# A gated short-convolution layer on one core: in-place scaling in the head, a folded -1/2, small products one chunk earlier, and a halved last store

## The chip, the core and the metric

The kernel runs on one core of a Trainium2 chip. The metric is the device time of one execution in microseconds (us), the median of several runs. Engines are named as the profile names them: PE is TensorE (matmuls; PEld its weight loads), DVE is VectorE, ACT is ScalarE, POOL is GpSimd, and SP is SyncE, which issues the DMAs. The engines run side by side; each works through its own instructions in the order in which the program lists them, and waits on semaphores of the others.

## The reference

With DEPTH = 1 only the first kind of layer runs, on x of 1024 rows by 1024 columns, in float32:

```
u  = x * rsqrt(mean(x*x) + 1e-6) * pre_norm
z, bg, cg, v = split(u @ w_in, 4)              # w_in: 1024 x 8192, each part 2048 wide
y  = bg * causal_conv3(cg * v, conv_w) * silu(z)
m  = y @ w_out                                 # w_out: 2048 x 1024
out = x + m * rsqrt(mean(m*m) + 1e-6) * post_norm
```

## The kernel before, in words

**Precision.** Each float32 operand is split into a high part (ScalarE, a rounding copy, L154) and a low part (VectorE, source minus high part, L155). A product of two operands is three matmuls: low by high, high by low, high by high (L188 to L190).

**Fewer products.** Both matrix products are cut into 2 x 2 blocks and done with seven block products instead of eight, called a to g. The sums of blocks that they need are made on POOL (`add_s`, L146 to L150, for the input weights: `se`, `sc`, `sf`, and `d` in place) and on VectorE and POOL for u. ScalarE and VectorE then split them.

**Chunks and pairs.** The first matmul is done in 16 chunks of 128 inner channels. A chunk c is two pairs, p = 2c (parts CG and V) and p = 2c + 1 (parts Z and BG), so chunk 2, the third, is pairs 4 and 5. For each pair the main loop (L790) issues products c, e, d, f of the pair, product a of the next pair, and g; the list `slots` (L742 to L757) holds the order. Up to chunk DEEP - 1 product b of the next pair also stands in it. From chunk DEEP on the two products b of a chunk are replaced by a second level of the same scheme: seven small products a' to g' of half the depth and 256 columns (`deep_product`, L670), spread among the others.

**What the small products need.** Once, the blocks of u's part b are rebuilt on POOL (`deep_parts`, L612, four adds of 512 columns), combined on POOL (`deep_subs`, L618, eight subtractions of 256) and split by ScalarE and VectorE (`deep_split`, L629: c', e', d', g'). The table `UNDER` (L760) says after which product each of these is issued. For each chunk POOL also makes four half sums of weights (`deep_sums`, L642), which `deep_prep` splits.

**Order of the work around it.** `prepare` (L780) issues the weight splits of every product that starts within LEAD = 7 us of the end of the current one, by a clock of 2.72 us a product and 0.72 a small one. `after` (L203) issues what follows a product: copies out of PSUM (`snap`, ScalarE), sums (VectorE: L212, L215, L220), SiLU, the gates (POOL: L217, L223, L225) and, at g, the last step of the convolution's input and the convolution (L236, L578, L581). Then come `add_s` of the next pair at e, d and f, the DMA loads `fetch(p + 2)` at d, and the entry of `UNDER`. Buffers are 36 pages of 128 x 512; the DMAs all go through SP's queue in program order.

**Head** (L410 to L470). The rows of x are eight tiles of 128. For each of the first four, ScalarE sums the squares, `rstd_start` and `rstd_finish` make 1/rms (a square root, a reciprocal and one Newton step: L103 to L111, with -1/2 times the reciprocal as an operation of its own, L105), and VectorE writes a diagonal matrix of it (`dg`, L420). TensorE turns the 128 x 128 blocks of the tile (L345) by a matmul with that diagonal, which scales in the same step. Some half tiles are scaled in place instead, by POOL (L425) and ScalarE (L433), and turned with the identity (L347). `high` and `low` (L357, L360) then read the turned blocks, times the norm's weight `gcol`, into the two parts of u_a and u_b. The first products (`plain`, L390 to L392) run on these without the seven-product scheme, with four turns of blocks between them. The second four tiles are squared, scaled in place (L468, L470) and turned later (`turn2`, L483). `rebuild` (L407) adds u's parts together on POOL. `stir` (L321) issues idle matmuls.

**Output** (L851 to L971). The second matmul runs in the same seven products over halves; rows of the result are normed, scaled with `gpost`, added to the residual `xr` (`finish`, L902) and stored, 256 KB at a time (L889).

Of the kernel before, what the change touches and what calls it, by code (L numbers as in the profile page):

```python
# [11 lines left out]
AF = mybir.ActivationFunctionType  # L12
ALU = mybir.AluOpType
EPS = 1e-6
WARM = 14
PAGES = 36
DEEP = 3
LEAD = 7.0


# [1 line left out]
def kernel(  # L22
# [16 lines left out]
    nc = tc.nc  # L39
    P = 128  # L40
    _, L, D = x.shape
    CI = w_out.shape[1]
    NT = L // P
    NK = D // P
    NC = CI // P
    HB = 512
    NE = D // HB
    TAPS = conv_w.shape[1]
    KH = NK // 2
    TH = NT // 2  # L50
# [4 lines left out]
    of = out.rearrange("b l d -> (b l) d")  # L55
# [12 lines left out]
    def bank(name):  # L68
        return psum.tile([P, HB], F32, tag="bank", name=name)

    def page(name, dtype=F32, shape=(HB,)):

        return pages.tile([P, *shape], dtype, tag="pg", name=name, bufs=PAGES)
# [4 lines left out]
    ident = const.tile([P, P], F32, tag="ident", name="ident")  # L78
# [16 lines left out]
    def rstd_finish(started, more=EPS):  # L95

        sd, ss, name, n = started

        def col(tag):
            return small.tile([P, n], F32, tag=f"{tag}{n}", name=f"{tag}_{name}")  # L100

        ve, r0, nt, hr, rs = (col(tag) for tag in ("ve", "r0", "nt", "hr", "rs"))
        nc.vector.tensor_scalar(ve, ss, more, None, op0=ALU.add)  # L103
        nc.vector.reciprocal(r0, sd)
        nc.vector.tensor_scalar(hr, r0, -0.5, None, op0=ALU.mult)  # L105
        if n == 1:
            nc.vector.scalar_tensor_tensor(nt, r0, ve, r0, op0=ALU.mult, op1=ALU.mult)
        else:
            nc.vector.tensor_mul(nt, r0, r0)
            nc.vector.tensor_mul(nt, nt, ve)  # L110
        nc.vector.scalar_tensor_tensor(rs, nt, 3.0, hr, op0=ALU.subtract, op1=ALU.mult)  # L111
        return rs


# [5 lines left out]
    def fetch(p, rows=(0, 1)):  # L120

        if p >= len(PAIRS):
            return
        c, tys = PAIRS[p]
        for n in rows:
            c0 = tys[n] * CI + c * P
            for k in (0, 1):
                if (p, n, k) not in raws:
                    raws[p, n, k] = page(f"raw_{p}_{n}{k}", shape=(KH, P))
                nc.sync.dma_start(raws[p, n, k], wiv[:, k * KH : (k + 1) * KH, c0 : c0 + P])  # L130
# [72 lines left out]
    def after(p, i):  # L203
# [22 lines left out]
        elif i == "g":  # L226
            if p % 2:
# [3 lines left out]
                y_done(c, cvs.pop(c))  # L231
            elif c < DEEP:
                start_conv(c)

    def start_conv(c, beside=lambda: None):
        nc.vector.tensor_mul(gpad[:, TAPS - 1 : TAPS - 1 + HB], banks[2 * c, "x"], sn[2 * c, "a"])  # L236
        conv(c, beside)
# [4 lines left out]
    def y_done(c, cv):  # L242
        nc.sync.dma_start(y_d[:, c], cv)
        done[c] = cv
# [54 lines left out]
    xs = [xa[:, t] for t in range(TH)] + [xb[:, t] for t in range(TH)]  # L299
# [2 lines left out]
    junk = page("junk", BF16, (D,))  # L302
    sq = small.tile([P, NT], F32, tag="sq", name="sq", bufs=1)
    gcol = small.tile([P, NK], F32, tag="gcol", name="gcol", bufs=1)
    dg = page("dg", shape=(TH, P))

    def load_x(t):
        nc.sync.dma_start(xs[t], xf[t * P : (t + 1) * P, :])
# [10 lines left out]
    def stir(n):  # L319
        for _ in range(n):  # L320
            nc.tensor.matmul(pw[:, :P], idle, idle, start=True, stop=True, skip_group_check=True)  # L321
# [16 lines left out]
    def turn(k, t):  # L338

        if (k, t // TH) not in pk:  # L340
            pk[k, t // TH] = bank(f"pk_{k}_{t // TH}")
        dst = pk[k, t // TH][:, t % TH * P : (t % TH + 1) * P]
        src = xs[t][:, k * P : (k + 1) * P]
        if t < 2 or t < TH and k < KH:
            nc.tensor.matmul(dst, src, dg[:, t], start=True, stop=True, skip_group_check=True)  # L345
        else:
            nc.tensor.transpose(dst, src, ident)  # L347

    def col(k):

        return xb[:, :, k * P : (k + 1) * P]
# [19 lines left out]
            plain_w[p, n, k] = [page(f"wn{n}{k}{h}_{p}", F32R) for h in "hl"]  # L371
            nc.scalar.copy(plain_w[p, n, k][0], block(p, n, k))

    def low_plain(p, n):
        for k in (0, 1):
            hi, lo = plain_w[p, n, k]
            nc.vector.tensor_sub(lo, block(p, n, k), hi.bitcast(F32))

# [32 lines left out]
    for t in range(TH):  # L411
        square(t)
        if t == 0:
            fetch(0)
            for t2 in range(TH, NT):
                load_x(t2)
            fetch(1)
            nc.sync.dma_start(cw_rows, conv_w[0].rearrange("t (c p) -> (t c) p", p=P))
        rs = pre_rstd([t])
        nc.vector.tensor_scalar(dg[:, t], ident, rs, None, op0=ALU.mult)  # L420
        for k in range(NK - 1 if t < 2 else KH):
            turn(k, t)
        late = xs[t][:, KH * P :]
        if t == 2:
            nc.gpsimd.tensor_scalar(late, late, rs, None, op0=ALU.mult)  # L425
        if t == 0:
            pg = pw[:, P : P + NK]
            nc.tensor.transpose(pg, grow, ident[:NK, :NK])
        if t == 1:
            nc.vector.tensor_copy(gcol, pg)  # L430
            stir(2)
    high_plain(0, 0)
    nc.scalar.activation(late, late, AF.Copy, scale=rs)  # L433
    low_plain(0, 0)

    def read_k(k):
        i, kk = "ab"[k // KH], k % KH
# [4 lines left out]
        read_k(k)  # L442
    high_plain(0, 1)
    low_plain(0, 1)
    fetch(2)
    for k in range(KH):
        plain(0, 0, 0, 0, [k], first=k == 0)
        for t in (2, 3) if k < KH - 1 else range(TH):
            turn(k + KH, t)
    read_k(4)  # L450
    square(TH)
# [157 lines left out]
    HH, KQ = HB // 2, KH // 2  # L609
    deep, deep_w = {}, {}  # L610

    def deep_parts(ks):  # L612

        for k in ks:
            deep[k] = page(f"deep{k}")
            nc.gpsimd.tensor_add(deep[k], UH["b"][:, k].bitcast(F32), UL["b"][:, k].bitcast(F32))

    def deep_subs(ks):  # L618

        for k in ks:  # L620
            (b11, b12), (b21, b22) = ((t[:, :HH], t[:, HH:]) for t in (deep[k], deep[k + KQ]))
            nc.gpsimd.tensor_sub(b12, b12, b11)
            nc.gpsimd.tensor_sub(b22, b22, b12)
            nc.gpsimd.tensor_sub(b11, b22, b11)
            nc.gpsimd.tensor_sub(b21, b21, b22)
# [117 lines left out]
    for p in range(2, len(PAIRS)):  # L743
        q = p + 1
        more = p // 2 >= DEEP
        sub = {"c": "a'", "e": "b'", "f": "c'", "a": "e'"} if p % 2 == 0 else {"c": "f'", "e": "d'", "f": "g'"}
# [4 lines left out]
        if q <= END:  # L751
            slots.append(("a", q))
            if more and p % 2 == 0:
                slots.append((sub["a"], p // 2))
            if q // 2 < DEEP:
                slots.append(("b", q))
# [1 line left out]


    UNDER = {  # L760
        ("c", 2 * DEEP - 2): lambda: deep_parts([0]),
        ("e", 2 * DEEP - 2): lambda: deep_parts([2]),
        ("d", 2 * DEEP - 2): lambda: deep_parts([1]),
        ("f", 2 * DEEP - 2): lambda: deep_parts([3]),
        ("g", 2 * DEEP - 2): lambda: deep_subs([0]),
        ("c", 2 * DEEP - 1): lambda: deep_subs([1]),
        ("a", 2 * DEEP): lambda: (deep_split("c'"), deep_split("e'")),
        ("g", 2 * DEEP - 1): lambda: deep_split("d'"),
        ("c", 2 * DEEP): lambda: deep_split("g'"),
# [3 lines left out]
    at, t = [], 0.0  # L773
# [78 lines left out]
    gpost = [page(f"gpost{e}") for e in range(NE)]  # L852
    for e in range(NE):
        nc.sync.dma_start(gpost[e], post_norm[:, e * HB : (e + 1) * HB].broadcast_to([P, HB]))
    gx = [page(f"gx{q}") for q in range(TH)]
    acc = p2.tile([P, 2, TH, HB], F32, tag="acc", name="acc")
    jk = p2.tile([P, HB], BF16, tag="jk", name="jk")
# [25 lines left out]
    def load_res(t):  # L883
        xr[t] = [page(f"xr{t}{e}") for e in range(NE)]
        for e in range(NE):
            nc.sync.dma_start(xr[t][e], xf[t * P : (t + 1) * P, e * HB : (e + 1) * HB])

    def store(t, e, src):
        nc.sync.dma_start(of[t * P : (t + 1) * P, e * HB : (e + 1) * HB], src)  # L889
# [12 lines left out]
    def finish(t):  # L902
        early = 0 if t < TH else 1
        late = 1 - early
        o, r = halves_of(t), xr[t]
        gl = gpost[late]
        ss, sl = sums_of[t], so[:, t, late : late + 1]
        sd = small.tile([P, 1], F32, tag="sd1", name=f"sd_post{t}")
        nc.scalar.activation(sd, sl, AF.Sqrt, bias=ss)
        if t < TH:  # L910
            rs = rstd_finish((sd, sl, f"post{t}", 1), ss)
            z = o[late]
            nc.vector.scalar_tensor_tensor(z, z, rs, gl, op0=ALU.mult, op1=ALU.mult)  # L913
            nc.gpsimd.tensor_add(z, z, r[late])  # L914
        else:
            z = gx[t - TH]
            nc.vector.tensor_mul(z, o[late], gl)
            rs = rstd_finish((sd, sl, f"post{t}", 1), ss)
            nc.vector.scalar_tensor_tensor(z, z, rs, r[late], op0=ALU.mult, op1=ALU.add)
            store(t, late, z)  # L920
        nc.vector.scalar_tensor_tensor(o[early], o[early], rs, r[early], op0=ALU.mult, op1=ALU.add)
        store(t, early, o[early])
        if t < TH:
            store(t, late, z)

# [18 lines left out]
            norm_square(q + TH, 0)  # L944

    def finish_row(t):
        finish(t)
        if t + 2 < NT:
            load_res(t + 2)

    for n, (i, h) in enumerate(OUT[:-2]):
        if (i, h) == ("f", 0):
# [43 lines left out]
```

## Time and profile before

| | us |
|---|---|
| median of 3 runs (788.2 to 788.76) | 788.74 |
| the profiled execution | 788.57 |
| its span | 786.8 |
| outside the span | 1.77 |
| PE busy in the span | 778.4 |
| DVE / POOL / ACT busy | 601.8 / 362.6 / 335.5 |

The page gives one execution: busy time by engine, the span in 40 slices with a busy digit each, the chain of work that ended last, and groups of instructions by line. A row of the timeline reads: start, length, engine, line, operation, output <- inputs, shape, count, and in brackets the engine's idle time before it with what ended it. A row of the chain of waits reads: start, time on the chain, engine, output and line, count. TensorE's rows overlap, since matmuls are pipelined: two neighbours of 0.39 us start 0.23 apart.

### The profile page before, as it was taken

The numbers are of one execution on the slowest core, as the hardware profiler recorded it, in microseconds if no ns is written. First come the engines' busy times: TensorE is split into PE (matmuls) and PEld (weight loads), VectorE is DVE, ScalarE is ACT, GpSimd is POOL, SyncE is SP. The second block draws the span as 40 slices with busy tenths as digits, with TensorE's granted clock in tenths as the row PEclk, the third lists the DMA queues.
The fourth block names the chain that finished last, engine by engine and source line by source line (L and its number), as shares of the span: only waits on it lengthen the run. The fifth ranks groups of instructions, "written<-read, shape, count | busy, mean of one in ns | idle before, by whom it ended". The sixth has DMA issues, their size and how long they took to land.

```text
span 786.8 us, 10799 instructions
## 1 busy us (share of the span) xinstructions
PE 778.4 (99%) x3728; PEld 654.3 (83%) x3728; DVE 601.8 (76%) x832; ACT 335.5 (43%) x610; POOL 362.6 (46%) x257
## 2 busy tenths in 40 slices
PE   9999999999999999999999999999999999999996
PEld 8888888888888888888888888888888888888885
DVE  6899757978787888889777878787868867744766
ACT  8564434433434343434243424243333547555441
POOL 2616579647474656656473838383837000000020
PEclk9999999999999999999999999999999999999999
DMA  9110431317070737464423323242415469983037
GB/s 334 43 54 11 138 93 55 108 41 230 24 254 1 253 125 238 146 242 144 138 95 107 107 94 110 92 141 60 147 55 190 171 211 394 406 287 108 0 112 263
DMA packets 108325, 114.50 MB, mean 146 GB/s; under 512 B 6584, under 2 KB 72176, under 8 KB 108272
## 3 DMA queue, kind: packets, MB, share of 16 engines
q1 hardware_dynamic: 108256, 113.82, 43.4%
q8 instruction: 29, 0.48, 0.2%
q14 instruction: 24, 0.20, 0.1%
q10 hardware_dynamic: 16, 0.00, 0.0%
HBM read 84.44 MB, written 29.36 MB: 145 GB/s over the span
## 4 chain that ended last, share of the span: by engine, by line
PE 98%; DVE 0%; DMA 0%; ACT 0%; issue 0%; DVEq 0%
PE px L188 14%; PE px L189 14%; PE px L190 14%; PE pv L188 7%; PE pv L189 7%; PE pv L190 7%; PE po_x L873 4%; PE po_x L872 4%; PE po_x L874 4%; PE po_v L873 2%; PE po_v L872 2%; PE po_v L874 2%; PE px L687 2%; PE px L685 2%; PE px L686 2%; PE pp L392 1%
## 5 line engine op out<-in xcount | busy, mean ns | idle before, releaser
L217 POOL TENSOR_TENSOR sne<-sne,cv 128x512 f32<-128x512 f32 x15 | 25.1, 1670 | 160.8 <-DVE sne L215 145.1
L914 POOL TENSOR_TENSOR acc<-acc,xr 128x512 f32<-128x512 f32 x4 | 6.5, 1618 | 132.3 <-DVE acc L913 130.9
L581 DVE SCALAR_TENSOR_TENSOR cv<-gpad,cw,cv 128x1024 f32<-128x1024 f32 x32 | 42.6, 1331 | 17.3 <-ACT cv L578 15.4
L155 DVE TENSOR_TENSOR wel<-se,weh 128x512 fp32r<-128x512 f32 x31 | 52.2, 1683 | 3.2 <-ACT weh L154 3.2
L146 POOL TENSOR_TENSOR se<-raw,raw 128x512 f32<-128x512 f32 x31 | 52.2, 1684 | 3.6 <-DMA raw<-in_sc_w_in 3.1
L150 POOL TENSOR_TENSOR sf<-raw,sc 128x512 f32<-128x512 f32 x31 | 53.0, 1711 | 0.0
L148 POOL TENSOR_TENSOR sc<-se,raw 128x512 f32<-128x512 f32 x31 | 50.1, 1616 | 2.4
L196 ACT COPY snc<-px 128x512 f32<-128x512 f32 x31 | 18.2, 586 | 73.4 <-PE px L190 70.0
L196 ACT COPY sna<-px 128x512 f32<-128x512 f32 x30 | 17.5, 582 | 73.2 <-PE px L190 48.9
L188 PE MATMUL pv<-u_e,wel 128*128 128x512 f32 x124 | 48.6, 392 | 0.0
L188 PE MATMUL px<-u_g,wgl 128*128 128x512 f32 x124 | 48.5, 391 | 0.0
L189 PE MATMUL pv<-u_e,weh 128*128 128x512 f32 x124 | 48.6, 392 | 0.0
L189 PE MATMUL px<-u_d,wdh 128*128 128x512 f32 x124 | 48.6, 392 | 0.0
L188 PE MATMUL px<-u_a,wal 128*128 128x512 f32 x124 | 48.6, 392 | 0.0
L189 PE MATMUL px<-u_a,wah 128*128 128x512 f32 x124 | 48.6, 392 | 0.0
L188 PE MATMUL px<-u_d,wdl 128*128 128x512 f32 x124 | 48.5, 391 | 0.0
L189 PE MATMUL px<-u_g,wgh 128*128 128x512 f32 x124 | 48.4, 390 | 0.0
L188 PE MATMUL pv<-u_f,wfl 128*128 128x512 f32 x124 | 48.3, 390 | 0.0
L188 PE MATMUL px<-u_c,wcl 128*128 128x512 f32 x124 | 48.2, 389 | 0.0
L190 PE MATMUL px<-u_g,wgh 128*128 128x512 f32 x124 | 48.2, 389 | 0.0
L190 PE MATMUL px<-u_a,wah 128*128 128x512 f32 x124 | 48.2, 389 | 0.0
L190 PE MATMUL px<-u_c,wch 128*128 128x512 f32 x124 | 48.2, 389 | 0.0
(367 smaller groups left out, 2486.9 us busy)
## 6 DMA issues: line engine op xcount, KB each, us to landing
raw<-in_sc_w_in SPq DMA_DIRECT2D x128, 256.0 KB, 4.0
y_d<-cv SPq DMA_DIRECT2D x16, 512.0 KB, 3.0
s_d<-s SPq DMA_DIRECT2D x32, 256.0 KB, 2.3
t<-in_sc_w_out SPq DMA_DIRECT2D x32, 256.0 KB, 4.2
t_d<-t SPq DMA_DIRECT2D x32, 256.0 KB, 2.6
s<-y_d SPq DMA_DIRECT2D x16, 256.0 KB, 3.8
xr<-in_x SPq DMA_DIRECT2D x16, 256.0 KB, 4.6
xa<-in_x SPq DMA_DIRECT2D x4, 512.0 KB, 5.2
```

Of the source, the lines that this page charges most:

```text
L146: nc.gpsimd.tensor_add(t, block(p, 1, 0), block(p, 1, 1))
L148: nc.gpsimd.tensor_sub(t, sums[p, "e"], block(p, 0, 0))
L150: nc.gpsimd.tensor_sub(t, block(p, 0, 1), sums[p, "c"])
L155: nc.vector.tensor_sub(lo, src, hi.bitcast(F32))
L188: nc.tensor.matmul(ps, lo, UH[i][:, k], start=first and k == 0, stop=False, skip_group_check=True)
L189: nc.tensor.matmul(ps, hi, UL[i][:, k], start=False, stop=False, skip_group_check=True)
L190: nc.tensor.matmul(ps, hi, UH[i][:, k], start=False, stop=last, skip_group_check=True)
L196: nc.scalar.copy(t, banks[p, "v" if i == "e" else "x"])
L581: nc.vector.scalar_tensor_tensor(cv, gpad[:, j : j + L], tap(c, j), cv, op0=ALU.mult, op1=ALU.add)
L872: nc.tensor.matmul(ps, lo, u[:, 0, k], start=first, stop=False, skip_group_check=True)
L873: nc.tensor.matmul(ps, hi, u[:, 1, k], start=False, stop=False, skip_group_check=True)
L874: nc.tensor.matmul(ps, hi, u[:, 0, k], start=False, stop=last, skip_group_check=True)
```

## The change

- In the head each of the first four tiles is multiplied by its 1/rms in place on VectorE (of the fourth tile the first half at once and the second half later, also on VectorE, in place of L433), and all blocks are turned with the identity. The diagonal `dg` and the scalings on POOL and ScalarE go. The third tile now has seven blocks turned at once instead of four, so fewer turns stand between the first products. Idle matmuls: one after tile 0, three after tile 1 (before: two after tile 1). The low part of weight block (0, 0, 1) is made after those of (0, 1).
- The operation `hr` of the Newton step goes; its -1/2 is in `gcol` and, by a scaling on POOL, in `gpost`.
- DEEP is 2 instead of 3: the third chunk has small products too. The adds of `deep_parts` are issued after f and g of pair 2, two each (before: one each after c, e, d and f of pair 4, which is two pairs later), the subtractions after c and e of pair 3 (before: after g of pair 4 and c of pair 5).
- The last row's last store is two halves, each stored as soon as it is summed; the residual loads of a later row are issued before the stores of the current one.

```diff
-DEEP = 3
+DEEP = 2
...
-        ve, r0, nt, hr, rs = (col(tag) for tag in ("ve", "r0", "nt", "hr", "rs"))
+        ve, r0, nt, rs = (col(tag) for tag in ("ve", "r0", "nt", "rs"))
-        nc.vector.tensor_scalar(hr, r0, -0.5, None, op0=ALU.mult)
-        nc.vector.scalar_tensor_tensor(rs, nt, 3.0, hr, op0=ALU.subtract, op1=ALU.mult)
+        nc.vector.scalar_tensor_tensor(rs, nt, 3.0, r0, op0=ALU.subtract, op1=ALU.mult)
...
-        if t < 2 or t < TH and k < KH:
-            nc.tensor.matmul(dst, src, dg[:, t], start=True, stop=True, skip_group_check=True)
-        else:
-            nc.tensor.transpose(dst, src, ident)
+        nc.tensor.transpose(dst, src, ident)
...
-        nc.vector.tensor_scalar(dg[:, t], ident, rs, None, op0=ALU.mult)
-        for k in range(NK - 1 if t < 2 else KH):
+        part = xs[t] if t < TH - 1 else xs[t][:, : KH * P]
+        nc.vector.tensor_scalar(part, part, rs, None, op0=ALU.mult)
+        for k in range(NK - 1 if t < TH - 1 else KH):
             turn(k, t)
-        late = xs[t][:, KH * P :]
-        if t == 2:
-            nc.gpsimd.tensor_scalar(late, late, rs, None, op0=ALU.mult)
         if t == 0:
+            stir(1)
...
         if t == 1:
-            nc.vector.tensor_copy(gcol, pg)
-            stir(2)
+            nc.vector.tensor_scalar(gcol, pg, -0.5, None, op0=ALU.mult)
+            stir(3)
     high_plain(0, 0)
-    nc.scalar.activation(late, late, AF.Copy, scale=rs)
-    low_plain(0, 0)
+    low_plain(0, 0, [0])
+    late = xs[TH - 1][:, KH * P :]
+    nc.vector.tensor_scalar(late, late, rs, None, op0=ALU.mult)
...
     low_plain(0, 1)
+    low_plain(0, 0, [1])
...
-        for t in (2, 3) if k < KH - 1 else range(TH):
+        for t in range(TH - 1 if k < KH - 1 else 0, TH):
             turn(k + KH, t)
...
-        ("c", 2 * DEEP - 2): lambda: deep_parts([0]),
-        ("e", 2 * DEEP - 2): lambda: deep_parts([2]),
-        ("d", 2 * DEEP - 2): lambda: deep_parts([1]),
-        ("f", 2 * DEEP - 2): lambda: deep_parts([3]),
-        ("g", 2 * DEEP - 2): lambda: deep_subs([0]),
-        ("c", 2 * DEEP - 1): lambda: deep_subs([1]),
+        ("f", 2 * DEEP - 2): lambda: deep_parts([0, 2]),
+        ("g", 2 * DEEP - 2): lambda: deep_parts([1, 3]),
+        ("c", 2 * DEEP - 1): lambda: deep_subs([0]),
+        ("e", 2 * DEEP - 1): lambda: deep_subs([1]),
...
+        nc.gpsimd.tensor_scalar(gpost[e], gpost[e], -0.5, None, op0=ALU.mult)
...
-        nc.vector.scalar_tensor_tensor(o[early], o[early], rs, r[early], op0=ALU.mult, op1=ALU.add)
-        store(t, early, o[early])
+        for cs in [slice(0, HB)] if t < NT - 1 else [slice(0, HH), slice(HH, HB)]:
+            a = o[early][:, cs]
+            nc.vector.scalar_tensor_tensor(a, a, rs, r[early][:, cs], op0=ALU.mult, op1=ALU.add)
+            nc.sync.dma_start(of[t * P : (t + 1) * P, early * HB + cs.start : early * HB + cs.stop], a)
...
     def finish_row(t):
-        finish(t)
         if t + 2 < NT:
             load_res(t + 2)
+        finish(t)
```

More of the change, by code (lines that the diff above doesn't have):

```diff
@@ L304 @@
     gcol = small.tile([P, NK], F32, tag="gcol", name="gcol", bufs=1)
-    dg = page("dg", shape=(TH, P))
     def load_x(t):
@@ L372, in high_plain, with low_plain @@
             nc.scalar.copy(plain_w[p, n, k][0], block(p, n, k))
-    def low_plain(p, n):
-        for k in (0, 1):
+    def low_plain(p, n, ks=(0, 1)):
+        for k in ks:
             hi, lo = plain_w[p, n, k]
```

## The prediction

> **What bounds the kernel now.** I read the page first, then the chain of waits, then the timeline of the head, of the third and fourth chunk and of the tail.
>
> ```profile
> PE 778.4 (99%) x3728; PEld 654.3 (83%) x3728; DVE 601.8 (76%) x832; ACT 335.5 (43%) x610; POOL 362.6 (46%) x257
> ...
> POOL 2616579647474656656473838383837000000020
> ...
> PE 98%; DVE 0%; DMA 0%; ACT 0%; issue 0%; DVEq 0%
> ...
> L581 DVE SCALAR_TENSOR_TENSOR cv<-gpad,cw,cv 128x1024 f32<-128x1024 f32 x32 | 42.6, 1331 | 17.3 <-ACT cv L578 15.4
> ```
>
> TensorE is the end of the chain in 98% of the span. So an edit counts only where it changes TensorE's first start, the matmul work, a wait of TensorE, or the tail after its last matmul. The sum is made against the profiled execution, 788.57 us (span 786.8, 1.77 around it); the median of the runs shown, 788.74, is 0.17 above it.
>
> **Head.** The chain of waits from 0 to 70 us (start, length):
>
> ```profile
> 6.48 0.30 DVE dg L420
> 6.82 1.83 PE pk L345 x14
> ...
> 11.01 1.33 PE pk L345 x10
> 12.36 0.70 ACT u_a L357
> 13.08 0.76 DVE u_a L360
> 13.89 0.50 PE pp L392
> ...
> 17.12 0.45 PE pk L345 x4
> ...
> 27.76 0.87 PE pk L347 x8
> ```
>
> A block turned against the diagonal is two matmuls and takes 1.83/7 = 0.26 us; a plain turn takes 0.87/8 = 0.11. And from the timeline, what in-place scaling costs and what covers it:
>
> ```profile
> 17.43 1.29 POOL L407 TENSOR_TENSOR xa<-u_a 128x512 f32<-128x512 f32 x1 [2.21 <-PE pk L345]
> 17.58 2.22 DVE L329 SCALAR_TENSOR_TENSOR u_e<-xb 128x1024 fp32r<-128x1024 f32 x1
> ...
> 21.71 1.21 DVE L329 SCALAR_TENSOR_TENSOR u_e<-xb 128x1024 fp32r<-128x1024 f32 x1
> ...
> 24.99 2.19 ACT L470 ACTIVATE xb<-xb,rs_pre 128x1024 f32<-128x1024 f32 x2 [1.41 <-DVE rs_pre L111]
> 24.99 1.42 DVE L468 TENSOR_SCALAR xb<-xb,rs_pre 128x1024 f32<-128x1024 f32 x2
> ```
>
> VectorE scales 1024 columns in 0.7 us (L468) where it now makes a diagonal in 0.3. Tile by tile: tile 0 is scaled from 6.41 (one -1/2 step of 0.07 less) to 7.16 and turned by 8.1; tile 1 from 7.87, turned by 9.6; tile 2, whose squares wait for its load, from 9.99, turned by 11.6. Tile 3's small steps queue behind that scaling on VectorE, so its half is scaled from 11.45 to 11.87 and its first block is turned at 12.2. ScalarE, rid of L433, starts u_a there, not at 12.36: -0.15. Behind it TensorE turns 7 blocks where it turned 10: three plain ones less, -0.33, and two diagonal ones (the 0.45 at 17.12) become plain, -0.23. Head: **-0.71**.
>
> Cover: the low step of the second weight block (0.6) moves behind the others on VectorE; queued behind it are u_b's low steps and the squares L329. Those squares take 2.22 where the later one takes 1.21, because they stand until POOL's rebuild at 17.43 is over; that rebuild waits for the last turn and comes 0.7 earlier, so the 0.6 fits in this wait. Without the cover it is a wait of TensorE of up to 0.6. At the next sync, the turns at 27.6, TensorE comes 0.7 earlier; ScalarE's scaling ends at 27.18, also up to 0.4 earlier: nothing, or 0.1. Head between -0.8 and 0.
>
> **Loop: what TensorE saves.** First matmul of product c in pairs 4, 6, 8 and 10:
>
> ```profile
> 103.27 0.39 PE L188 MATMUL px<-u_c,wcl 128*128 128x512 f32 x1
> ...
> 138.63 0.39 PE L188 MATMUL px<-u_c,wcl 128*128 128x512 f32 x1
> ...
> 176.63 0.39 PE L188 MATMUL px<-u_c,wcl 128*128 128x512 f32 x1
> ...
> 214.41 0.39 PE L188 MATMUL px<-u_c,wcl 128*128 128x512 f32 x1
> ```
>
> The third chunk's 13 products between the first two rows take 35.36, 2.72 each; with its product b in the pair before it costs 38.08. The fourth, the first with small products, takes 38.00; the fifth 37.78. So small products save 0.30 a chunk, and the first such chunk lost 0.22 in waits. If nothing else moved: third chunk 37.78 for 38.08, fourth 37.78 for 38.00, **-0.52** and the waits of the new transition, S.
>
> **Loop: what the transition costs.** The four adds (L616) and eight subtractions (L622 to L625) on POOL come one chunk earlier, and a product b (2.72) no longer lies between them and their use. They go where POOL has its only room, and its sums for pair 4 stand behind them:
>
> ```profile
> 79.01 1.78 DVE L155 TENSOR_TENSOR wcl<-sc,wch 128x512 fp32r<-128x512 f32 x1
> ...
> 80.20 1.74 POOL L150 TENSOR_TENSOR sf<-raw,sc 128x512 f32<-128x512 f32 x1
> 85.05 1.30 POOL L146 TENSOR_TENSOR se<-raw,raw 128x512 f32<-128x512 f32 x1 [3.11 <-DMA raw<-in_sc_w_in]
> 86.42 1.29 POOL L148 TENSOR_TENSOR sc<-se,raw 128x512 f32<-128x512 f32 x1
> 93.36 1.68 POOL L217 TENSOR_TENSOR sne<-sne,cv 128x512 f32<-128x512 f32 x1 [5.64 <-DVE sne L215]
> ...
> 123.14 0.74 POOL L622 TENSOR_TENSOR deep<-deep 128x256 f32<-128x256 f32 x1
> ```
>
> The first row is a low step of VectorE: 0.68 alone (wfl below), 1.78 while POOL works, and POOL's next sum took 1.74 for 1.29. They take turns: a VectorE step with two SBUF inputs stands until the POOL operation in flight ends (1.25 of the 1.29 for 512 columns, 0.7 for 256), and the next POOL operation stands until that step ends (1.74 - 1.25 = 0.5; a step of the convolution 1.15, of the 1.33 that the page's L581 has with its waits). What it did in the fourth chunk, on VectorE and then TensorE:
>
> ```profile
> 135.29 0.86 DVE L155 TENSOR_TENSOR dw0l<-raw,dw0h 128x512 fp32r<-128x512 f32 x1 [1.21 <-ACT dw0h L154]
> ...
> 137.78 2.40 DVE L155 TENSOR_TENSOR ucl_deep<-deep,uch_deep 128x256 fp32r<-128x256 f32 x2
> 140.10 1.84 DVE L155 TENSOR_TENSOR u_b<-deep,u_b 128x256 fp32r<-128x256 f32 x2
> 141.85 1.23 DVE L155 TENSOR_TENSOR wdl<-raw,wdh 128x512 fp32r<-128x512 f32 x1
> ...
> 144.71 2.94 DVE L155 TENSOR_TENSOR udl_deep<-deep,udh_deep 128x256 fp32r<-128x256 f32 x2
> 147.58 0.68 DVE L155 TENSOR_TENSOR wfl<-sf,wfh 128x512 fp32r<-128x512 f32 x1
> 148.18 0.75 DVE L155 TENSOR_TENSOR ugl_deep<-deep,ugh_deep 128x256 fp32r<-128x256 f32 x2
> ...
> 148.41 0.47 PE L188 MATMUL pv<-u_f,wfl 128*128 128x512 f32 x1
> ```
>
> Two steps of 256 columns, 0.75 together alone (the last VectorE row), took 1.8 to 2.9. wfl ended at 148.26, 9.63 after product c, just when product f was due (three products of 2.72 to 2.75 and two small ones of 0.71 after c); f began 0.14 late. There was no slack.
>
> I replay the new order with these lengths, on the old clock; up to 81.94 (end of sf) nothing differs. POOL: four adds among wel, wdl and two convolution steps, to 89.1; four subtractions among wfl, wal and wgl, to 94.3; then se and sc of pair 4, to 96.8 (today 87.7). ScalarE's high part wch waits for sc, VectorE's wcl for wch, and in VectorE's order L220 stands behind wcl, in ScalarE's the SiLU behind L220, and dw0h behind that. So dw0l, today 3.34 before its chunk's product c, starts at 100.05 with product c now at 103.27 - 2.72 = 100.55, half a microsecond before it: 2.8 late. POOL has then L217, d's sum, L223, f's sum, four half sums and the next pair's three ahead, two operations more than in the fourth chunk at this point, and VectorE's small steps take turns with them:
>
> ```
> VectorE: dw0l 100.6, wel 102.3, c' 105.4, e' 107.9, wdl 109.1, d' 112.7, wfl 114.5   (ends)
> TensorE: d wanted at 107.4, starts 109.15; f wanted at 111.9, starts 114.55
> ```
>
> Waits: 1.7 + 2.65 + 0.1 for the next step = S = 4.5. Where wcl loses the race for its first turn by 0.05, the same replay gives 6.1. From below S is 0 where POOL is through in time. I take 4.5. Loop: -0.52 + 4.5 = **+4.0**.
>
> **Tail and the rest.** The last row's steps, and the end (columns of the last three: stretch, length, engines, granted clock, DMA share, GB/s):
>
> ```profile
> 781.74 0.15 DVE L105 TENSOR_SCALAR hr_post<-r_post 128x1 f32<-128x1 f32 x1
> 781.81 0.21 DVE L107 SCALAR_TENSOR_TENSOR nt_post<-r_post,ve_post 128x1 f32<-128x1 f32 x1
> ...
> 783.00:784.00 1.00, 0.00 (x0) 0.00 (x0) 0.66 (x1) 0.00 (x0) 0.00 (x0) 0.73 0.12 49
> 784.00:784.50 0.50, 0.00 (x0) 0.00 (x0) 0.00 (x0) 0.00 (x0) 0.00 (x0) 0.50 1.04 406
> 784.50:785.00 0.50, 0.00 (x0) 0.00 (x0) 0.00 (x0) 0.00 (x0) 0.00 (x0) 0.50 0.99 381
> ```
>
> Without the -1/2 step the next starts 0.07 sooner: **-0.07**. The store in two: both last stores, 512 KB, already leave back to back at some 400 GB/s with every queue full, so a last half issued no earlier ends no earlier: 0, between -0.35 (half a transfer) and +0.15 (one more step and issue). The scaling of the norm's weights on POOL is two operations where the page's digits show it idle; the residual loads issued ahead of the stores are done with before the last row. Both nothing; uncovered they would delay rows that are not the last.
>
> Sum: -0.71 + 4.0 - 0.07 = **+3.2**; on the median 788.74 that is **792.0 us**.
>
> **The rivals.**
> *The deep steps fit* (the other side: a gain). S stays below 0.8 if POOL is done with pair 4's sums by about 94, as it would if VectorE's steps did not take a POOL operation each. For it: POOL's idle 3.11 and 5.64 above. Against: 12 operations of 9.9 us go into it and the rows show strict turns. Then 788.74 - 0.71 - 0.30 - 0.07 = 787.7.
> *Half of the wait.* VectorE wins some turns, S about 2: 789.4.
> [...]
>
> **How the numbers follow.** Forecast, S from 3 to 6.5: 0.58. The deep steps fit: 0.24. Half of the wait: 0.12. Clock: 0.06. A measurement here tells about 0.2% (1.6 us) from no change. Slower by more is the forecast and the clock, 0.64; within 0.2% is half of the wait and most of the fit, 0.31; faster by more, below 787.16, is the fit with a better tail and head, 0.05. The forecast's own range is 790.3 to 794. The range for 8 in 10 must reach into the gain: 787.5 to 794.2, which leaves out some 0.08 on either side.
>
> **What would show it.** Right: TensorE idle before product d and product f of pair 4, released by wdl and wfl; sc of pair 4 on POOL near 95, not 86; dw0l after product a of pair 4 has long ended; u_a near 12.2; later chunks at 37.78. Wrong: product c of pair 8 only 75.6 (two times 37.78) after that of pair 4; or matmuls of 0.45 spacing after 13 us, which would be the clock.

## The result and the profile after

| | before | after |
|---|---|---|
| median, us | 788.55 (788.2 to 788.99, 6 runs) | 794.39 (793.83 to 795.94, 6 runs) |
| ratio, 95% interval | | 1.0076 [1.0063, 1.0089] |
| profiled execution, us | 788.57 | 794.52 |
| span / outside it, us | 786.8 / 1.77 | 792.5 / 2.02 |

The changed kernel is slower by 0.76%, 5.84 us. The forecast was 792.0 in a range of 787.5 to 794.2: the sign and the place were right, the size was 2.4 us too small, and the time lies 0.2 above the range.

The page of the changed kernel: busy time, the chain that ended last by engine, and one group (last columns: busy us, mean ns, idle time before it with what ended most of it).

```profile
PE 778.5 (98%) x3726; PEld 653.8 (82%) x3726; DVE 608.2 (77%) x828; ACT 336.0 (42%) x611; POOL 370.0 (47%) x262
...
PE 92%; POOL 3%; DVE 3%; issue 1%; DMA 1%; ACT 1%; SPq 0%; DVEq 0%; POOLq 0%
...
L187 PE MATMUL pv<-u_f,wfl 128*128 128x512 f32 x124 | 48.9, 395 | 3.4 <-DVE wfl L154 3.4
```

PE's share of the chain fell from 98% to 92%: VectorE, POOL and ScalarE now stand on it, and the group names where: TensorE waits once, 3.4 us, for wfl. Its timeline at that place and at the later chunks (product a of pair 4; c, d and f of pair 4; c of pairs 6 and 8):

```profile
94.52 0.39 PE L187 MATMUL px<-u_a,wal 128*128 128x512 f32 x1
...
100.20 0.50 PE L187 MATMUL px<-u_c,wcl 128*128 128x512 f32 x1
...
108.19 0.47 PE L187 MATMUL px<-u_d,wdl 128*128 128x512 f32 x1 [0.81 <-ACT dw1h L153]
...
114.54 0.47 PE L187 MATMUL pv<-u_f,wfl 128*128 128x512 f32 x1 [3.37 <-DVE wfl L154]
...
144.40 0.39 PE L187 MATMUL px<-u_c,wcl 128*128 128x512 f32 x1
...
182.18 0.39 PE L187 MATMUL px<-u_c,wcl 128*128 128x512 f32 x1
```

From c to c: the third chunk takes 144.40 - 100.20 = 44.20, the fourth 37.78, and so the fifth, as forecast for chunks with small products and no wait. All that is lost lies in the third. From product a of pair 4 to c of pair 8 it is 182.18 - 94.52 = 87.66, before 176.63 - 95.11 = 81.52: +6.14. With the head (94.52 for 95.11, -0.59) and the tail (from the end of the last matmul to the end of the span 6.87 for 6.72, +0.15) that is the span's +5.7.

The same stretch on VectorE and on POOL:

```profile
99.18 0.85 DVE L154 TENSOR_TENSOR dw0l<-raw,dw0h 128x512 fp32r<-128x512 f32 x1 [1.21 <-ACT dw0h L153]
...
101.65 2.94 DVE L154 TENSOR_TENSOR ucl_deep<-deep,uch_deep 128x256 fp32r<-128x256 f32 x2
104.51 2.40 DVE L154 TENSOR_TENSOR u_b<-deep,u_b 128x256 fp32r<-128x256 f32 x2
106.83 1.22 DVE L154 TENSOR_TENSOR wdl<-raw,wdh 128x512 fp32r<-128x512 f32 x1
...
109.81 2.91 DVE L154 TENSOR_TENSOR udl_deep<-deep,udh_deep 128x256 fp32r<-128x256 f32 x2
112.64 1.75 DVE L154 TENSOR_TENSOR wfl<-sf,wfh 128x512 fp32r<-128x512 f32 x1
```

```profile
81.32 6.93 POOL L612 TENSOR_TENSOR deep<-u_b 128x512 f32<-128x512 f32 x4
88.21 1.73 POOL L618 TENSOR_TENSOR deep<-deep 128x256 f32<-128x256 f32 x1
...
94.70 1.29 POOL L147 TENSOR_TENSOR sc<-se,raw 128x512 f32<-128x512 f32 x1
```

wfl ends at 114.39 and product f starts 0.15 later; sc, from which the rest follows, comes at 94.70 on POOL. Read VectorE's rows also for what stands between: three splits of 256 columns (c', e', d') take 8.25 us ahead of wdl and wfl.

The view by stretches, from the end of product d to c' (length; busy time of PE, PEld, DVE, ACT, POOL; granted clock; DMA share; GB/s):

```profile
111.00:114.50 3.50, 0.16 (x1) 0.00 (x0) 3.50 (x4) 0.62 (x1) 2.76 (x3) 1.00 0.99 286
114.50:116.00 1.50, 1.46 (x4) 1.20 (x5) 1.50 (x5) 0.62 (x1) 0.00 (x0) 0.65 0.99 294
...
117.00:118.00 1.00, 1.00 (x4) 0.81 (x3) 1.00 (x2) 0.00 (x0) 0.00 (x0) 0.50 0.00 0
118.00:119.00 1.00, 1.00 (x5) 0.79 (x5) 1.00 (x3) 0.00 (x0) 0.00 (x0) 0.83 0.00 0
```

This is what the forecast did not have: TensorE stands for 3.4 us, and then the granted clock is half for more than 3 us, just while product f runs. f takes 4.40 (114.54 to 118.94) where it takes 2.75.

### The profile page after: what moved, and what is told of

It is laid out like the page before. It is cut to its first block, busy times and chain, and to the rows that moved or that the text cites. A ratio compares the mean times of both kernels' runs of the same rounds, so it can differ in the third digit from the quotient of the medians.

```text
span 792.5 us, 10806 instructions
## 1 busy us (share of the span) xinstructions
PE 778.5 (98%) x3726; PEld 653.8 (82%) x3726; DVE 608.2 (77%) x828; ACT 336.0 (42%) x611; POOL 370.0 (47%) x262
## 4 chain that ended last, share of the span: by engine, by line
PE 92%; POOL 3%; DVE 3%; issue 1%; DMA 1%; ACT 1%; SPq 0%; DVEq 0%; POOLq 0%
PE px L187 13%; PE px L188 13%; PE px L189 13%; PE pv L187 7%; PE pv L188 7%; PE pv L189 7%; PE po_x L868 4%; PE po_x L869 4%; PE po_x L867 4%; PE po_v L868 2%; PE po_v L869 2%; PE po_v L867 2%; PE px L683 2%; PE px L681 2%; PE px L682 2%
## 5 line engine op out<-in xcount | busy, mean ns | idle before, releaser
L189 PE MATMUL pv<-u_f,wfh 128*128 128x512 f32 x124 | 49.0, 395 | 0.0
L188 PE MATMUL pv<-u_f,wfh 128*128 128x512 f32 x124 | 48.9, 394 | 0.0
L188 PE MATMUL px<-u_a,wah 128*128 128x512 f32 x124 | 48.6, 392 | 0.0
```

The source lines that it names most:

```text
L188: nc.tensor.matmul(ps, hi, UL[i][:, k], start=False, stop=False, skip_group_check=True)
L189: nc.tensor.matmul(ps, hi, UH[i][:, k], start=False, stop=last, skip_group_check=True)
```

## The experiments

Theory: the small products from the third chunk cost it all, by late splits on VectorE, and 1.65 us of it is the clock behind the wait. Rivals: something else in the change costs (the shifted head, the halved store), or POOL is simply too full there. The kernel before ran beside each group: 788.75 (first four), 788.53 (next four), 788.62 (next three), 788.71 (last). 

**1. Small products back to the fourth chunk,** the rest of the change kept: `DEEP = 3` and the old entries of `UNDER`.

> The changed kernel with DEEP = 3 and the old table of deep steps: head, weights and stores stay changed. Theory (the loss is the deep steps' queue on POOL in the third chunk, its waits and the half clock behind them): no wait of TensorE in the third chunk, the old wait of 0.22 in the fourth; 788.55 - 0.6 (head) + 0.2 (tail) = 788.1. Rival (the new head or the stores carry part of the loss): above 789.

Measured 788.09, ratio 0.9992 [0.9983, 1.0002]; no wait of TensorE in the loop is left in the view of its waits. As the theory said: without this part the change costs nothing.

**2. Small products from the third chunk alone,** in the kernel before: `DEEP = 2` and the new entries.

> The kernel before with only DEEP = 2 and the new table. Theory: the whole loss of the loop, -0.5 + 6.7 of waits and half clock, 788.55 + 6.1 = 794.7. Rival (the waits need the new head, which shifts TensorE against POOL by 0.6): 3 us or less above the kernel before, below 791.5.

Measured 794.78, ratio 1.0072 [1.0055, 1.0088]. TensorE's waits:

```profile
PE pv L188 <- DVE wfl L155: 3.4, 1, 3.4
...
PE px L188 <- ACT dw1h L154: 0.8, 1, 0.8
```

The same two waits as in the changed kernel, with the old head and the old tail: this part alone is the loss.

**3. The rebuilding of the blocks on VectorE** instead of POOL:

```diff
-            nc.gpsimd.tensor_add(deep[k], ...)
+            nc.vector.tensor_add(deep[k], ...)
...
-            nc.gpsimd.tensor_sub(b12, b12, b11)
+            nc.vector.tensor_sub(b12, b12, b11)
```

and so for all twelve.

> The changed kernel with the four adds and eight subtractions of u's part b on VectorE instead of POOL. Theory (POOL's queue): sc of pair 4 is back near 87, dw0l some 3 us before product c, waits of TensorE under 0.7 in all and no half clock: 787.7 to 788.5. Rival (VectorE's own order and load is what is late, and POOL only looks so): VectorE gets some 5 us more work, the waits stay or grow, 794 or more.

Measured 790.21, ratio 1.0024 [1.0014, 1.0035]: between the two, a miss for both. POOL has sc at 85.89 now, 8.8 us earlier, and the wait before d is gone; f still waits 2.1. VectorE's order shows why:

```profile
101.56 2.40 DVE L154 TENSOR_TENSOR ucl_deep<-deep,uch_deep 128x256 fp32r<-128x256 f32 x2
103.88 1.85 DVE L154 TENSOR_TENSOR u_b<-deep,u_b 128x256 fp32r<-128x256 f32 x2
...
108.50 2.91 DVE L154 TENSOR_TENSOR udl_deep<-deep,udh_deep 128x256 fp32r<-128x256 f32 x2
111.34 0.68 DVE L154 TENSOR_TENSOR wfl<-sf,wfh 128x512 fp32r<-128x512 f32 x1
```

With POOL's share taken away, c', e' and d' still stand ahead of wfl and still take 7.2 us, where 0.75 for each two in the kernel before would be 2.25, in turns with the sums that POOL makes meanwhile (pair 4's for f, the half sums, and the next pair's). And the clock fell behind this shorter pause too:

```profile
109.90:112.00 2.10, 0.12 (x1) 0.00 (x0) 2.10 (x4) 0.49 (x1) 1.24 (x1) 1.00 0.99 276
112.00:113.00 1.00, 0.84 (x4) 0.73 (x5) 1.00 (x5) 0.74 (x3) 0.00 (x0) 1.00 1.09 310
...
114.00:115.00 1.00, 1.00 (x3) 0.72 (x3) 1.00 (x3) 0.00 (x0) 0.00 (x0) 0.50 0.80 228
```

This profiled execution took 791.86, at a mean granted clock of 0.995; two more of the eight took 791.46 and 792.07 at 0.995 and 0.997, and the other five 789.46 to 790.39 at 0.997 to 0.999. The middles of the two groups lie 1.85 apart, about what the fall costs, so the clock may have held in the five; only this one execution has a trace, so that is not shown.

**4. The pause filled:** ten idle matmuls between products d and f of pair 4.

```diff
+        if (i, p) == ("f", 4):
+            fill = bank("fill")
+            for _ in range(10):
+                nc.tensor.matmul(fill[:, :P], idle, idle, start=True, stop=True, skip_group_check=True)
```

> The changed kernel with ten idle matmuls issued between product d and product f of pair 4, in TensorE's wait. Theory (the 3.6 us pause lets the granted clock drop, and product f runs at half speed): the wait for wfl stays, product f takes 2.75 instead of 4.40, granted clock 1.0 throughout: 794.39 - 1.65 = 792.7. Rival (product f is slow for another reason, such as its operands): f stays at 4.4 and the time at 794.4.

Measured 793.1, ratio 1.0057 [1.0042, 1.0072].

```profile
111.22 2.39 PE L798 MATMUL fill<-idle 128*128 128x128 f32 x20
114.77 0.47 PE L187 MATMUL pv<-u_f,wfl 128*128 128x512 f32 x1 [1.15 <-DVE wfl L154]
...
117.57 0.28 PE L681 MATMUL px<-uch_deep,dw1l 128*128 128x256 f32 x1
```

f starts as late as before, but takes 2.80 (114.77 to 117.57) at a granted clock of 1.00. The wait and the clock behind it are two costs, and the second is 1.3 us in the medians, 1.6 in the traces.

**5. POOL's steps in their old spread** (the entries of `UNDER` before, with `DEEP = 2`), so that they begin at 71 instead of 81.

> The changed kernel, small products from the third chunk as there, but the POOL steps go back to their old spread: the four adds after products c, e, d and f of pair 2, the subtractions after g of pair 2 and c of pair 3. Theory (they come too late on POOL for the sums of pair 4 behind them): the adds start some 8 us earlier, POOL's sc of pair 4 ends near 90 us instead of 96, product d of pair 4 does not wait and product f waits under 0.5 us, the clock does not fall: 787.9 to 789. Rival (one chunk early there is not enough room on POOL and VectorE wherever the steps stand): the waits move to pair 3 or to products d and f of pair 4 and stay over 3 us: over 791.5.

Measured 792.59, ratio 1.0056 [1.0041, 1.0072]: the rival. On POOL the twelve steps and pair 3's sums now stand in one unbroken row from 71 to 95, most adds taking 1.75, where one takes 1.29, in turns with VectorE, and all eight subtractions instead of four come ahead of pair 4's sums. sc ends at 97.93, later than in the changed kernel (95.99), and then the waits move to ScalarE's order. The largest now stands before c, which the rival had not named:

```profile
97.96 0.62 ACT L153 CAST wch<-sc 128x512 fp32r<-128x512 f32 x1 [8.00 <-POOL sc L147]
...
101.93 0.58 ACT L195 COPY sna<-px 128x512 f32<-128x512 f32 x1
```

```profile
PE px L187 <- ACT sna L195: 2.9, 1, 2.9
PE pv L187 <- ACT wch L153: 1.1, 1, 1.1
```

Product c needs the PSUM bank that the copy at 101.93 empties, and the copy stands behind wch, which waited for sc. My count of 8 us gained had left out that POOL would not get faster by starting sooner.

**6. The four splits later in VectorE's program,** POOL's steps untouched:

```diff
-        ("a", 2 * DEEP): lambda: (deep_split("c'"), deep_split("e'")),
-        ("g", 2 * DEEP - 1): lambda: deep_split("d'"),
-        ("c", 2 * DEEP): lambda: deep_split("g'"),
+        ("c", 2 * DEEP): lambda: deep_split("c'"),
+        ("e", 2 * DEEP): lambda: deep_split("e'"),
+        ("d", 2 * DEEP): lambda: deep_split("d'"),
+        ("f", 2 * DEEP): lambda: deep_split("g'"),
```

> The changed kernel with only the four splits of the rebuilt blocks moved later in the program (c' after c, e' after e, d' after d, g' after f of pair 4, instead of c' and e' after a, d' after g of pair 3, g' after c). wdl and wfl then have no split of 256 columns ahead of them on VectorE. Theory, with VectorE's order as the holder of wdl and wfl: the two splits before wdl took 5.3 us in its queue, so d starts on time and f waits under 1 us: near 788.5. Theory, with POOL's sums sd and sf (each behind sc at 96) as the holder: sf of pair 4 ends at 105.7, the split of it at 108, so f still fits, which gives the same; so a wait of f over 2 us here would say that the small products themselves, now fed later, wait in place of it: 791 to 794.

Measured 789.4, ratio 1.001 [1.0001, 1.0019]. VectorE, and TensorE's only wait in the loop:

```profile
103.03 1.11 DVE L154 TENSOR_TENSOR wdl<-raw,wdh 128x512 fp32r<-128x512 f32 x1 [1.84 <-ACT wdh L153]
...
105.98 1.01 DVE L154 TENSOR_TENSOR wfl<-sf,wfh 128x512 fp32r<-128x512 f32 x1
106.91 1.84 DVE L154 TENSOR_TENSOR ucl_deep<-deep,uch_deep 128x256 fp32r<-128x256 f32 x2
```

```profile
PE pv L681 <- DVE sna L692: 0.9, 1, 0.9
```

wfl ends 7.4 us earlier than in the changed kernel (0.55 of it from an earlier load in the head, of which below), and c', which is due after f, is still in time. Five of the 5.84 us are gone by the order of four splits alone. The edit moves ScalarE's high parts of these splits too, but they were not what held d and f: in the changed kernel wdh was made by 103.52 and wfh by 106.39, and VectorE came to wdl at 106.83 and to wfl at 112.64. POOL's twelve steps are as late as ever (sc at 94.16): they make the stretch tight, the splits' place makes it a wait.

**7. The changed order one chunk later** (`DEEP = 3` with the new entries).

> The changed kernel with DEEP back at 3 but the new order of POOL's steps relative to it: adds after f and g of pair 4, two each, subtractions after c and e of pair 5, so that they stand as far ahead of their use as in the changed kernel, but a chunk later. Theory (distance to the use decides, the chunk does not): the waits before d and f of pair 6 are as large as those of pair 4, S of 4 to 7 us, with a fall of the clock behind the wait: 792 to 795. Rival (the early chunk is special, its POOL and VectorE are fuller): S under 1, 788 to 789.

Measured 792.27, ratio 1.0046 [1.0032, 1.006]. f of pair 6 waits 2.8 for wfl, and the clock falls again:

```profile
148.20:151.00 2.80, 0.04 (x2) 0.06 (x1) 2.80 (x3) 0.62 (x1) 2.08 (x2) 1.00 1.00 270
...
153.00:154.00 1.00, 1.00 (x4) 0.81 (x3) 1.00 (x4) 0.09 (x1) 0.00 (x0) 0.50 0.01 3
```

So the order and the distance to the use cost most of it, 4.2 us over experiment 1's kernel. The early chunk is not needed for a wait, but it adds to it: there the same steps cost 6.3, with a wait of 0.8 before d as well.

**8 and 11. The last store whole again,** on the kernel of experiment 1, in two groups:

```diff
-        for cs in [slice(0, HB)] if t < NT - 1 else [slice(0, HH), slice(HH, HB)]:
+        for cs in [slice(0, HB)]:
```

> The changed kernel with small products from the fourth chunk and the old order of POOL's steps (the first experiment's kernel, 788.09), and the last store whole again. Theory (the halved store costs one more step and one more issue): the time from the last matmul to the end falls by 0.2 us, from 6.87 to 6.65, 0.07 below the kernel before: 787.9. Rival (the halves are free, the longer tail is noise of one trace): the tail stays 6.85 or so and the time 788.1. The medians can hardly tell these two; the tails in the traces can.

> The kernel with small products from the fourth chunk, the old order and the whole last store once more, to stand on the same chip beside the two kernels with small products from the third chunk: 787.7 to 788.0 where before is at 788.5. If small products one chunk earlier are worth 0.30 us of TensorE and no wait eats it, the two others are at or below this one; if the transition costs more than 0.3 wherever it stands, this one stays the fastest.

Measured 787.74, ratio 0.9993 [0.9984, 1.0002], and 787.94, ratio 0.9988 [0.9979, 0.9997]. The last store's issue on SP's queue, first of the changed kernel, then of experiment 8, and with it the last matmul of each:

```profile
785.23 0.39 PE L869 MATMUL po_x<-ou_g,oy_g 128*128 128x512 f32 x1
...
788.95 0.87 SPq L919 DMA_DIRECT2D out<-c  x2
```

```profile
778.68 0.39 PE L871 MATMUL po_x<-ou_g,oy_g 128*128 128x512 f32 x1
...
782.63 0.33 SPq L921 DMA_DIRECT2D out<-c  x1
```

From the last matmul's start to the end of the issue: 4.59 halved, 4.28 whole (4.35 in the kernel before, which has the extra step hr). The second of two halves is issued 0.31 later than one whole. It is so in all the traces of the new tail: 4.58 to 4.61 in the seven with halves, 4.28 in the five with the whole store (two here, three below). From the last matmul to the end of the span experiments 1 and 3 to 7, with the halved store, took 6.82 to 6.88, these two 6.73 and 6.65. Experiment 2, with the old tail and a whole store, took 4.59 to the end of the issue as well, since VectorE paused 0.27 there before the last rows were scaled; so a single trace would not have settled it.

**9. Splits later still:** c' after c, e' after e of pair 4, d' after c, g' after d of pair 5; store whole.

> The changed kernel (small products from the third chunk) with the four splits still later, c' after c and e' after e of pair 4, d' after c and g' after d of pair 5, and the last store whole. In the run with later splits one wait of 0.9 us was left, before f' of pair 5, for a sum that stood on VectorE behind the splits of d' and g' (1.5 us). Theory (VectorE's program order is all that holds the small products back): that wait goes, and with 0.2 of the store the time is 789.4 - 0.95 - 0.2 = 788.25, between 787.9 and 788.5. Rival (the splits now come too late for d' and g' themselves, or POOL's turns make another wait of the same size): 789 or more, with a wait of 0.9 or more before f', d' or g' in pair 5.

Measured 792.67, ratio 1.0048 [1.0035, 1.0062]: the rival. The wait before f' is gone, but g' now waits itself, 2.1 us in two pieces, and the clock falls behind it (product a of pair 6 takes 4.34, from 134.78 to 139.12, in rows of 0.63 instead of 0.39):

```profile
128.83 2.61 DVE L577 SCALAR_TENSOR_TENSOR cv<-gpad,cw,cv 128x1024 f32<-128x1024 f32 x2 [1.22 <-ACT cv L574]
...
132.56 1.83 DVE L154 TENSOR_TENSOR ugl_deep<-deep,ugh_deep 128x256 fp32r<-128x256 f32 x2
```

The split of g' landed behind the convolution, due at 131.5 and begun at 132.56.

**10. The same with the rebuilding on VectorE.**

> The same as the kernel with the still later splits, with the adds and subtractions of the rebuilt blocks on VectorE instead of POOL, as in the third experiment. Theory: the third experiment's remaining wait before f (2.1 us) and its fall of the clock came from the splits ahead of wfl in VectorE's order, so here no wait of TensorE over 0.5 us is left between pairs 4 and 6 and the time is that of the kernel with POOL's steps or up to 0.3 less: 787.6 to 788.3. Rival (twelve more operations, some 6 us, are too much for VectorE in pairs 2 and 3): a wait before f of pair 4 of over 1 us, 789.5 or more.

Measured 790.0, ratio 1.0024 [1.0013, 1.0035]: the time lies in the rival's range, its wait before f did not come. f is on time: VectorE's order was what held it in experiment 3. But g' waits 1.7 here, in two pieces of 0.89 and 0.80, and the clock falls behind even these (rows of 0.63 instead of 0.39):

```profile
133.85 0.39 PE L682 MATMUL px<-ugl_deep,dw 128*128 128x256 f32 x1 [0.80 <-DVE ugl_deep L154]
...
134.19 0.63 PE L187 MATMUL px<-u_a,wal 128*128 128x512 f32 x1
```

Product a of pair 6 takes 4.34 (134.19 to 138.53) where it takes 2.72.

**12. Splits in between:** c' after c, e' after e, d' after g of pair 4, g' after c of pair 5; store whole.

> The kernel with later splits with the splits of d' and g' placed between the two orders tried: c' after c, e' after e and d' after g of pair 4, g' after c of pair 5 (in the run with later splits d' and g' stood after d and f of pair 4 and pushed f' by 0.9; in the next one they stood after c and d of pair 5, and g' itself came 2.1 late), the last store whole. Theory (only the place of these splits in VectorE's program order decides): no wait of TensorE over 0.4 us between pairs 4 and 6, no fall of the clock, and 788.6 - 0.71 (head) - 0.52 (loop) - 0.07 (Newton step) + 0.25 (the start of product c of pair 4) = 787.5, between 787.2 and 787.9; the time of the kernel with small products from the fourth chunk is 787.7 to 787.9. Rival (there is no place on VectorE without a wait, because POOL's turns leave no slack in this transition): some wait of 0.5 or more before f', d' or g' in pair 5, 788.3 or more.

Measured 788.37, ratio 0.9993 [0.9984, 1.0002]. No wait of the loop stands among TensorE's waits, as the theory had it; the time is 0.9 above its 787.5 and in the rival's range, so a hit for the waits and a miss for the time. The loop's part of that: from product a of pair 4 (95.00) to c of pair 8 (176.51) 81.51, where 81.25 was expected. c starts 0.25 late, behind the copy of its bank,

```profile
100.06 0.58 ACT L195 COPY sna<-px 128x512 f32<-128x512 f32 x1
...
100.69 0.19 PEld L187 LDWEIGHTS px<-u_c,wcl 128*128 128x128 f32 x1 [0.52 <-ACT sna L195]
```

and 0.26 more goes in gaps too short for the view of the waits. 81.51 is what the kernel before takes (81.52), and the kernels of experiments 1, 8 and 11 (81.53 to 81.58). The best order found for the third chunk gives back all that the small products save there, and the kernel of experiments 8 and 11 (787.74 and 787.94) stays the fastest made here.

## Why the prediction was wrong

Its steps one by one, in us of the profiled execution:

| step | forecast | measured |
|---|---|---|
| head | -0.71 | -0.59 |
| third and fourth chunk at 37.78 | -0.52 | -0.52 |
| S: start of c, and c to a' | 0 | 0.37 |
| S: wait before d | 1.7 | 0.96 |
| S: wait before f | 2.65 | 3.60 |
| S: clock behind the wait | 0 | 1.65 |
| S: the rest | 0.1 | 0.08 |
| tail | -0.07 | +0.15 |
| outside the span | 0 | +0.25 |
| sum | +3.2 | +5.95 |

**The step that failed is S, taken as 4.5 and measured as 6.66.** Its waits were right in sum (4.56 for 4.35) and place, and its releaser too: f by wfl; the row of d names dw1h, which came last by the profile, with wdl's end at 108.05, 0.14 before d's start. What S lacked is the price of the wait itself: 1.65 us of product f at half the clock. The row for it was in the prediction, the 0.73 and 0.50 behind the last matmul, but I took it up for the head alone, where a fall had a chance of 0.06 and did not occur. And my reading of that row, half a clock some 3.4 us after the last matmul (its end at 780.06, half a clock from 783.46, worked out from the 0.73), would have spared waits of 1.7 and 2.65; the traces show falls behind shorter pauses (2.8 and 2.1 us in experiments 7 and 3, 1.30 and 0.80 in 9, 0.89 and 0.80 in 10). Experiment 4 takes this term alone away. The rest of what S lacked is 0.37 at the start of c and 0.21 in the two waits together. That sum came out better than its parts, 0.74 too much and 0.95 too little: f starts when wfl ends, so whatever d does not wait, f waits. The other replay, 6.1, would have given 793.6, and no such term either.

**What holds the waits** was told too simply. The forecast put it on POOL's twelve steps ahead of pair 4's sums. Experiment 3 frees POOL of them and f still waits; experiment 6 leaves them and f does not wait. The replay had the splits of c', e' and d' in VectorE's order, with their turns, and so gave nearly the right waits; the sentence drawn from it named one of two causes. Each is needed: without POOL's share 4.2 of the 5.84 us are gone (experiment 3, where VectorE has the twelve steps to do besides), without the early splits 5.0 (experiment 6).

**Head.** u_a began at 12.27, forecast 12.2, and the last 0.1 went in the later sync, where it had been allowed for. **Tail.** The Newton step gave its 0.07; the halved store cost 0.2 where I took nothing, and +0.15 was the end of its bound.

**Rivals.** That the deep steps fit came true in no kernel with the changed order; with the splits in between (experiment 12) S was 0.51, and the time 788.37 for the 787.7 of that rival. Half of the wait (S of 2) did not come about, nor a fall of the clock in the head: between 6.99 and 12.56 us TensorE did 25 turns of 128 columns, one small one and only eight records of idle matmuls, and the granted clock was 1.00 in every stretch of 1 us. Of the signs that were named: sc near 95 (94.70), dw0l after the end of product a (99.18, a ended by 97.24), later chunks at 37.78: all as forecast.

## What to carry to other kernels

A wait of TensorE can cost more than its length: behind pauses of 1.7 to 3.4 us in all at one place of the loop, in one piece or two, the clock fell in five of six traces. Add what a product of 2.75 us loses at half clock, 1.3 to 1.65 us here, or fill the pause with idle matmuls. When steps are moved ahead by one round, move what consumes them to its own due time as well, and not past it (experiment 9): on an engine that works in program order, splits that nobody needs yet stood before the two that TensorE waited for, and their order was worth 5 us. And ask first what a perfect transition would bring: 0.52 us here, of which the best order found gave back 0.51.

## What the runs showed of the hardware

**Half a clock is not decided by the length of the pause alone.** It fell in five traces: after pauses of 3.4 us (changed kernel), 2.8 (experiment 7) and 2.1 (experiment 3), and after two short ones, 1.30 and 0.80 (experiment 9) and 0.89 and 0.80 (experiment 10). Experiment 2, with the same pause of 3.4, has a mean granted clock of 0.995, experiment 1 of 0.998. It did not fall behind this one of 2.9 in the profiled execution of experiment 5, whose mean is 0.998 (the other three have 0.994 and 0.995):

```profile
99.50:102.50 3.00, 0.20 (x1) 0.00 (x0) 1.79 (x3) 2.14 (x5) 2.73 (x3) 1.00 0.00 0
102.50:104.00 1.50, 1.44 (x6) 1.23 (x7) 1.50 (x2) 1.50 (x6) 1.50 (x1) 1.00 0.05 11
```

The half clock begins 0.3 to 1.4 us after the end of the last pause, and in each of the five it lasts some 3.4 us. In the changed kernel and experiments 3 and 7 that is worked out from the granted clock in stretches of 0.5 to 1.5 us, in 9 and 10 from TensorE's rows, which are 0.63 long instead of 0.39, as in the changed kernel at a granted clock of 0.50. What decides whether it falls, no run here shows.

**The third tile's load sets the head.** ScalarE's squares of that tile wait for it, and u_a follows; first the changed kernel, then experiment 9:

```profile
7.79 1.06 ACT L324 ACTIVATE junk<-xa 128x1024 bf16<-128x1024 f32 x1 [0.81 <-DMA xa<-in_x]
...
12.27 2.42 ACT L352 ACTIVATE u_a<-pk,gcol 128x512 fp32r<-128x512 f32 x4 [0.56 <-PE pk L342]
```

```profile
7.14 1.06 ACT L324 ACTIVATE junk<-xa 128x1024 bf16<-128x1024 f32 x1 [0.26 <-DMA xa<-in_x]
...
11.60 2.43 ACT L352 ACTIVATE u_a<-pk,gcol 128x512 fp32r<-128x512 f32 x4 [0.56 <-PE pk L342]
```

That row begins between 7.14 and 8.20 from kernel to kernel, and product a of pair 4 starts 86.69 to 86.84 after it in the twelve profiled kernels with the new head, 87.30 and 87.35 in the two with the old. So the head's gain is 0.6 us, and up to 1 us of difference between two executions comes in with the first loads (experiments 8 and 11, the same kernel: product a at 94.11 and 94.74): two heads are compared from that load on, not from the span's start.
